# Sample attention of a four-layer encoder step: score products issued as one row, new keys as a 128-key block

## The chip, the core and the metric

The program runs on one core of a Trainium2 chip. The core has a matrix engine (TensorE: PE in the profile, with its weight loads as PEld), three engines for elementwise work (VectorE: DVE, ScalarE: ACT, GpSimd: POOL) and a queue that issues the DMA transfers (SyncE: SP). Each engine works through its own instructions in the order in which the program lists them and waits on semaphores. The metric is the device time of one execution in microseconds; lower is better.

## What is computed

One inference step of four transformer layers of width 2048, for 256 prompt tokens and for 8 batch elements with 16 new tokens each ("sample"). Layer i mixes by kind i mod 3: band attention with sinks (A, layers 0 and 3), latent attention (B, layer 1), chunk-band attention (C, layer 2). Beside the mixer, every layer has a 4-head cross-attention into 256 memory tokens. The sample half attends to cached keys and to the 16 new keys of its own batch element:

```python
def attend(q, k, v, bias, valid, sink):
    s = jnp.einsum("bqhgd,bkhd->bhgqk", qg, k) * (d ** -0.5)
    if bias is not None:
        s = s + bias
    ...
    p = jax.nn.softmax(s, axis=-1)      # kind A adds the sink to the denominator
    return jnp.einsum("bhgqk,bkhd->bqhgd", p, v)

# kinds A and C, sample: cached keys first, then the new ones
out = attend(q, concat([past_k, k], axis=1), concat([past_v, v], axis=1), bias_fn(rel), None, sink)
y = x + (concat([out, cross]) * silu(gate)) @ w_out
```

The numbers of cached keys are 128 (A), 512 (B and C) and 256 (cross).

## The kernel before

All large products (`proj_nat`, `proj_tr`) split both operands into two parts and run three products of 128 contraction rows by 128 columns of weights each. Their weights come by DMA (`raw_*`), are split by ACT (`whi_*`, L149) and DVE (`wlo_*`, L150), two buffers of each, and go to PE. The program is written as a data flow with tiles and pools; a planner decides, before the kernel is built, in which order each engine gets its instructions, so that attention work and large products alternate on PE. Pools bound how far things run ahead: `kcT` (transposed keys) has four buffers, `prs` (scores and probabilities, one row per query and head) two, `cch` (cached keys and values) five, the PSUM bank `s` one.

TensorE can be addressed in parts. A product with 32 queries as weights (`128*32` in the profile: 128 contraction rows, 32 columns) takes a quarter of the array's columns; which quarter follows from where the result starts in PSUM (`s[32 * h:32 * h + 32]`). With 32 contraction rows (`32*32`, `32*64`, `32*128`) it also takes a quarter of the rows. A product of two fp32 operands shows as two MATMUL instructions.

The sample attention, for each kind:

- **C** (`layer_c`, L695 to L740): three groups of four heads, eight batch elements, 24 blocks in all. Per block: for each head four transposes of cached keys (L707) into `ktp`, a copy to `kcT` (DVE for even heads, ACT for odd ones) and directly behind it that head's score product (L714); then softmax; four transposes of the probabilities `pt`; the new keys' probabilities; 16 products with the cached values (L734) and four with the new ones (L737); one transpose of the result. Where the next group's projections or the gate products are ready, the planner puts them between.
- **A** (`sample_a`, two layers, two pairs of key heads, four pairs of batch elements: 16 blocks). Eight score products with 64 columns of queries (`128*64`), half with 128 cached keys and half with 16 new ones; two transposes of probabilities; products with values for each of two batch elements and two key heads: cached (L597), then new (L598).
- **B** (`sample_b`, eight batch elements, two halves of the heads): 96 rows of queries and heads, 512 cached latents, and the new ones at L1059 and L1067.
- **Cross** (`cross`, L440 to L472): 16 blocks of two batch elements, per element four score products of 256 keys (L451).

The new keys of batch elements 2n and 2n+1 share 32 partitions (16 each) of the tiles that hold all eight elements' new values (`vn[:, 2]`, `c_s`). `new_block` (L387) lays a block of 32 probabilities next to the cached ones, the 16 of the own element and 16 zeros for the neighbour (POOL memset, L392). Those 32 columns are turned into rows by a product with the identity (`mm(o[vr, P:256], blk, ident)`, L587, L727, L1059), which writes the 32 partitions `vr` where the new values lie, and the product with the new values has 32 contraction rows (`ptn[vr]` by `vn[vr]`, L598, L737, L1067).

Of the kernel before, what the change touches and what calls it, by code (L numbers as in the profile page):

```python
# [10 lines left out]
F32 = mybir.dt.float32  # L11
# [48 lines left out]
def encoder_step(ctx: ExitStack, tc: tile.TileContext, ins: dict, outs: list, layers=(0, 1, 2, 3)):  # L60
# [73 lines left out]
    # ---------------------------------------------------------------- products  # L134
# [65 lines left out]
    # ---------------------------------------------------------------- residual stream  # L200
# [28 lines left out]
    # column k of the residual stream, transposed, and its squares  # L229
# [27 lines left out]
    # ---------------------------------------------------------------- memory keys and values  # L257
# [50 lines left out]
    # ---------------------------------------------------------------- attention, prompt  # L308
# [19 lines left out]
    def attn_band(nm, qk, v0, v1, bm, sink, dst, mul=False):  # L328
# [6 lines left out]
        pr = sm.tile([P, 544], F32, tag="prs", name=f"pr_{nm}")  # L335
# [21 lines left out]
    def attn_full(nm, q, k, v0, v1, dst, mul):  # L357
        s = atb(f"s_{nm}", "o")
        for t in range(2):
            mm(s[:, t * 256:(t + 1) * 256], q[:, t * P:(t + 1) * P], k)  # L360
        nmx = tiny.tile([P, 4], F32, tag="nm", name=f"nm_{nm}")
        nc.vector.tensor_reduce(nmx[:, :2], s.rearrange("p (t k) -> p t k", t=2), AX.X, ALU.max, negate=True)
        pr = sm.tile([P, 544], F32, tag="prs", name=f"pr_{nm}")
# [52 lines left out]
    def cross(l, xqT, oT, mul=False):  # L416
# [23 lines left out]
        for b2 in range(NB // 2):  # L440
# [13 lines left out]
            pr = sm.tile([P, 544], F32, tag="prs", name=f"pr_{nm}")  # L454
# [19 lines left out]
    # ---------------------------------------------------------------- gate and output projection  # L474
# [8 lines left out]
    # silu(2u) = u (1 + tanh u), rbc holds half the scale  # L483
# [62 lines left out]
    # ---------------------------------------------------------------- layers  # L546
    def sample_a(l, j, p2, qs, kT, vn, sink_r, oT):
# [7 lines left out]
        for b2 in range(4):  # L555
            nm = f"as{l}{p2}{b2}"
            vr = slice(32 * b2, 32 * b2 + 32)
# [6 lines left out]
            pr = sm.tile([P, 544], F32, tag="prs", name=f"pr_{nm}")  # L564
            bl = []
            for i in range(2):
                b = 2 * b2 + i
                bl.append(new_block(pr[:, i * 160:(i + 1) * 160], P, b))
                po, no = (0, P) if i == 0 else (DS, 0)
                for jj in range(2):  # L570
# [3 lines left out]
                    mm(s[rows, i * 144 + po:i * 144 + po + P], q, kcT[:, (2 * i + jj) * P:(2 * i + jj + 1) * P])  # L574
                    mm(s[rows, i * 144 + no:i * 144 + no + DS], q, kT[:, kv, SP0 + DS * b:SP0 + DS * (b + 1)])
            nmx = tiny.tile([P, 4], F32, tag="nm", name=f"nm_{nm}")
            for i in range(2):
                bo = DS if i == 0 else 0
                nc.vector.tensor_tensor_reduce(out=bl[i][3], in0=s[:, i * 144:(i + 1) * 144], in1=bm_a[:, p2, bo:bo + 144],
                                               scale=-1.0, scalar=sink_r[:, 2 + p2:3 + p2], op0=ALU.add, op1=ALU.min,  # L580
                                               accum_out=nmx[:, i:i + 1])
# [7 lines left out]
            nc.scalar.copy(pts[:, 0:256], pt[:, 0:256])  # L589
            nc.vector.tensor_copy(pts[vr, 256:512], pt[vr, 256:512])  # L590
            o = atb(f"o_{nm}", "o")
            for i in range(2):
                for jj in range(2):
                    kv = 2 * p2 + jj
                    c0 = i * P + 64 * jj
                    oo = o[64 * jj:64 * jj + 64, i * P:(i + 1) * P]
                    mm(oo, pts[:, c0:c0 + 64], vcs[b2 // 2][:, 2 * (b2 % 2) + i, jj * P:(jj + 1) * P], True, False)  # L597
                    mm(oo, pts[vr, 256 + c0:256 + c0 + 64], vn[vr, 2, kv * P:(kv + 1) * P], False, True)  # L598
# [59 lines left out]
    def layer_c(l, xt, rx, xres, last):  # L658
# [3 lines left out]
        for g in range(3):  # L662
# [32 lines left out]
            for b in range(NB):  # L695
# [6 lines left out]
                vr = slice(32 * (b // 2), 32 * (b // 2) + 32)  # L702
                s = atb(f"s_{nm}", "s")
                for h in range(4):
# [9 lines left out]
                    mm(s[32 * h:32 * h + 32, :], q, kcT)  # L714
                pr = sm.tile([P, 544], F32, tag="prs", name=f"pr_{nm}")
                past, new, blk, span = new_block(pr, 512, b)
# [13 lines left out]
                ptn = sm.tile([P, P], F32, tag="ptn", name=f"ptn_{nm}", bufs=1)  # L730
                nc.vector.tensor_copy(ptn[vr], o[vr, P:256])
                for kt in range(4):
                    for h in range(4):
                        mm(o[32 * h:32 * h + 32, 0:P], pts[:, kt * P + 32 * h:kt * P + 32 * h + 32],  # L734
                           vc[kt // 2][:, kt % 2, h * P:(h + 1) * P], kt == 0, False)
                for h in range(4):
                    mm(o[32 * h:32 * h + 32, 0:P], ptn[vr, 32 * h:32 * h + 32], vn[vr, 2, h * P:(h + 1) * P], False, True)  # L737
# [5 lines left out]
    # ---------------------------------------------------------------- latent attention  # L743
# [12 lines left out]
    def layer_b(l, xt, rx, xres, last):  # L756
# [7 lines left out]
        # new latents and rotary keys  # L764
# [30 lines left out]
        # query latents, memory queries, gates  # L795
# [27 lines left out]
        # [latent half][head half]: batch, head, position  # L823
# [6 lines left out]
        def two_heads(qc):  # L830
# [21 lines left out]
            # absorbed sample queries  # L852
# [29 lines left out]
            # keys and values of two heads  # L882
# [62 lines left out]
        # key products, only for the norms of the cached keys  # L945
# [13 lines left out]
        # one row per head to one row per head and query  # L959
# [52 lines left out]
        def sample_b(b, rk, ch, cl, raw, krT):  # L1012
            nm = f"bs{b}"
            vr = slice(32 * (b // 2), 32 * (b // 2) + 32)
# [18 lines left out]
            ptn = qkp.tile([P, 1552], F32, tag="kT", name=f"ptn{nm}")[vr, 0:192]  # L1033
            for hf in range(2):
# [12 lines left out]
                pr = sm.tile([P, 544], F32, tag="prs", name=f"pr_{nm}{hf}")  # L1047
                past, new, blk, span = new_block(pr[:96], 512, b)
# [11 lines left out]
                mm(pt[vr, 384:480], blk, ident[:96, :96])  # L1060
                nc.scalar.copy(ptb[:, :, hf * 96:(hf + 1) * 96], pt[:, 0:384].rearrange("p (t r) -> p t r", t=4))
                nc.vector.tensor_copy(ptn[:, hf * 96:(hf + 1) * 96], pt[vr, 384:480])
# [11 lines left out]
        # scores of the new latents: 32 keys of two batch elements at a time, of which the own ones are kept  # L1074
# [48 lines left out]
    # ---------------------------------------------------------------- gains and biases  # L1123
# [6 lines left out]
    def setup():  # L1130
# [13 lines left out]
        # relative-position biases: one row per head over rel in descending order  # L1144
# [16 lines left out]
        # every head's row once per query, so that a row pitch of one less shifts it by one per query  # L1161
# [10 lines left out]
        bm_a = cst.tile([P, 2, 160], F32, name="bm_a")  # L1172
        nc.gpsimd.memset(bm_a, 0.0)
        for p2 in range(2):
            for j in range(2):
                r, h0 = slice(j * 64, j * 64 + 48), 6 * p2 + 3 * j
                nc.sync.dma_start(out=bm_a[r, p2, DS:160], in_=toeplitz(sh_a, h0, 127, [[LA * 64, 3], [LA - 1, DS], [1, 144]]))
                nc.sync.dma_start(out=bm_a[r, p2, 0:DS], in_=toeplitz(sh_a, h0, 255, [[LA * 64, 3], [LA - 1, DS], [1, DS]]))
# [19 lines left out]
    # ---------------------------------------------------------------- run  # L1198
# [63 lines left out]
```

## Time and profile before

| | |
|---|---|
| median of 3 runs | 2983.43 us (2979.32 to 2983.58) |
| profiled execution, first to last instruction | 2979.2 us |
| PE busy | 2945.2 us, 99% of the span |
| DVE, ACT, POOL busy | 1351.6, 1315.1, 422.8 us |
| DMA engines busy, mean | 46.4% |
| granted TensorE clock, mean | 0.996 of full speed |

In the rows of the timeline below, a line is one instruction or several equal ones in a row (xN): its start, the time until the last of them ends, engine, line, operation, tile written<-tiles read, and the form rows*columns of the array with the size of the moving operand. Ends of matmuls are modelled and overlap with what follows, so what one line costs PE is read from its start to the start of the next line.

### The profile page before, as it was taken

To read this page: it belongs to the slowest core of one execution; us is meant where nothing else is said; L and a number is where in the kernel's file an instruction comes from. 1 tells how busy PE (TensorE), PEld (TensorE's weight loads), DVE (VectorE), ACT (ScalarE), POOL (GpSimd) and SP (SyncE) were. 2 spreads that over 40 slices of the span, in tenths; PEclk is the share of its full clock that TensorE was granted. 3 is DMA by queue.
4 is the path that set the end of the run, shared out by engine and by line. 5 is a ranking of instruction groups with operands and counts; after the bars stand their busy time and mean duration, and the time that the engine had idled before them with its cause. 6 is when DMAs were issued, how large, how long until landed. Compare 5 with 4: busy or idle time off the path is not lost.

```text
span 2979.2 us, 44016 instructions
## 1 busy us (share of the span) xinstructions
PE 2945.2 (99%) x17178; PEld 2499.4 (84%) x17178; DVE 1351.6 (45%) x2521; ACT 1315.1 (44%) x2819; POOL 422.8 (14%) x437
## 2 busy tenths in 40 slices
PE   8989999999999999999999999999999999999999
PEld 6867888899989987888898877777889987888987
DVE  5544445453434455555443443343445344345433
ACT  6555355333444365444334453434334344553332
POOL 1100111011100063333011110010101111010100
PEclk9999999999999999999999999999999999999999
DMA  7785553354444622001444546655566444532343
GB/s 256 240 271 184 169 163 100 113 184 149 147 131 121 186 78 61 16 23 56 162 149 131 163 158 215 203 175 197 175 198 223 149 138 128 189 108 89 111 163 130
DMA packets 314830, 446.82 MB, mean 150 GB/s; under 512 B 20833, under 2 KB 183666, under 8 KB 314622
## 3 DMA queue, kind: packets, MB, share of 16 engines
q1 hardware_dynamic: 314622, 444.01, 46.4%
q8 instruction: 135, 2.21, 0.3%
q14 instruction: 73, 0.60, 0.1%
HBM read 412.48 MB, written 34.69 MB: 150 GB/s over the span
## 4 chain that ended last, share of the span: by engine, by line
PE 96%; DMA 2%; DVE 1%; ACT 1%; SPq 0%; issue 0%; DVEq 0%; ACTq 0%
PE pt_g L90 18%; PE pt_o L90 13%; PE pn_aq L90 7%; PE kpkn L90 5%; PE pn_o L90 4%; PE pn_m L90 4%; PE pn_xq L90 4%; PE pn_cq L90 3%; PE pn_ck L90 3%; PE pn_cv L90 3%; PE pn_ak L90 2%; PE pn_av L90 2%; PE s_cs L90 2%; PE ktpcs L103 2%; PE o_as L90 2%; PE o_cs L90 1%
## 5 line engine op out<-in xcount | busy, mean ns | idle before, releaser
L90 PE MATMUL pt_g<-xt_x,whi_g 128*128 128x384 f32 x2048 | 534.4, 341 | 0.0
L90 PE MATMUL pt_o<-og,whi_o 128*128 128x384 f32 x1536 | 379.2, 334 | 0.0
L90 PEld LDWEIGHTS pt_g<-xt_x,whi_g 128*128 128x128 f32 x2048 | 367.8, 188 | 13.2 <-issue 11.6
L90 PE MATMUL pt_g<-xt_x,wlo_g 128*128 128x384 f32 x1024 | 343.4, 343 | 0.0
L150 DVE TENSOR_TENSOR wlo_o<-raw_o,whi_o 128x1024 fp32r<-128x1024 f32 x128 | 157.7, 1232 | 262.9 <-ACT whi_o L149 259.4
L90 PEld LDWEIGHTS pt_o<-og,whi_o 128*128 128x128 f32 x1536 | 276.3, 188 | 0.2 <-issue 0.2
L149 ACT CAST whi_o<-raw_o 128x1024 fp32r<-128x1024 f32 x128 | 134.6, 1052 | 278.9 <-PE pt_o L90 148.6
L90 PE MATMUL pt_o<-og,wlo_o 128*128 128x384 f32 x768 | 245.6, 335 | 0.0
L150 DVE TENSOR_TENSOR wlo_g<-raw_g,whi_g 128x1024 fp32r<-128x1024 f32 x128 | 160.4, 1253 | 176.7 <-ACT whi_g L149 171.3
L149 ACT CAST whi_g<-raw_g 128x1024 fp32r<-128x1024 f32 x128 | 134.3, 1049 | 183.8 <-PE pt_g L90 154.6
L90 PEld LDWEIGHTS pt_g<-xt_x,wlo_g 128*128 128x128 f32 x1024 | 191.9, 188 | 7.7 <-issue 6.8
L90 PE MATMUL pn_aq<-whi_aq,xt_x 128*128 128x512 f32 x576 | 186.2, 399 | 0.0
L90 PE MATMUL pn_m<-whi_m,xt_m 128*128 128x512 f32 x512 | 161.6, 395 | 0.4 <-ACT whi_m L154 0.4
L90 PEld LDWEIGHTS pt_o<-og,wlo_o 128*128 128x128 f32 x768 | 143.2, 188 | 0.0
L90 PE MATMUL kpkn<-wk,chkn 128*128 128x384 f32 x512 | 133.5, 343 | 0.0
L155 DVE SCALAR_TENSOR_TENSOR wlo_m<-raw_m,gc_mem,whi_m 128x512 fp32r<-128x512 f32 x128 | 97.6, 803 | 76.0 <-ACT whi_m L154 76.0
L90 PEld LDWEIGHTS pn_aq<-whi_aq,xt_x 128*128 128x128 f32 x576 | 107.0, 188 | 22.5 <-issue 0.8
L90 PE MATMUL pn_xq<-whi_xq,xt_x 128*128 128x512 f32 x384 | 122.0, 395 | 0.5 <-ACT xt_x L214 0.5
L90 PE MATMUL pn_o<-whi_o,og 128*128 128x512 f32 x384 | 119.6, 391 | 0.0
L90 PE MATMUL pn_aq<-wlo_aq,xt_x 128*128 128x512 f32 x288 | 115.2, 401 | 0.0
L90 PEld LDWEIGHTS pn_m<-whi_m,xt_m 128*128 128x128 f32 x512 | 95.8, 189 | 21.1 <-ACT whi_m L154 1.1
L154 ACT ACTIVATE whi_m<-raw_m,gc_mem 128x512 fp32r<-128x512 f32 x128 | 85.8, 716 | 58.6 <-PE pn_m L90 58.2
(502 smaller groups left out, 5974.9 us busy)
## 6 DMA issues: line engine op xcount, KB each, us to landing
raw_o<-in_w_out_dram SPq DMA_DIRECT2D x128, 512.0 KB
raw_m<-in_w_mem_kv_dram SPq DMA_DIRECT2D x64, 512.0 KB
raw_g<-in_a_w_in_dram SPq DMA_DIRECT2D x64, 512.0 KB
raw_aq<-in_a_w_in_dram SPq DMA_DIRECT2D x48, 512.0 KB
kccs<-in_cache_c_k_dram SPq DMA_DIRECT2D x48, 512.0 KB
vccs<-in_cache_c_v_dram SPq DMA_DIRECT2D x48, 512.0 KB
kxs<-in_cache_mem_k_dram SPq DMA_DIRECT2D x32, 512.0 KB
vxs<-in_cache_mem_v_dram SPq DMA_DIRECT2D x32, 512.0 KB
```

The costliest lines, as they stand in the source:

```text
L90: nc.tensor.matmul(out, lhsT=lhsT, rhs=rhs, start=start, stop=stop)
L103: nc.tensor.transpose(out, in_, ident[:k, :k])
L149: nc.scalar.copy(hi[:, :, :ncols], r)
L150: nc.vector.tensor_tensor(lo[:, :, :ncols], r, hi[:, :, :ncols].bitcast(F32), ALU.subtract)
L154: nc.scalar.activation(hi[:, i, :ncols], r[:, i, :], AF.Copy, scale=g)
L155: nc.vector.scalar_tensor_tensor(lo[:, i, :ncols], r[:, i, :], g, hi[:, i, :ncols].bitcast(F32), ALU.mult, ALU.subtract)
```

## The change

- A helper `mm_row` issues a list of products so that all of them come behind the first on PE. The cross-attention and kind C put the last head first (its keys are transposed last); in C, the four score products of a block are now issued after all four transposes and copies. The products with the values and A's scores go through it as well.
- `new_block` now makes a block of 128 columns behind the cached keys: all of it is filled (POOL memset of 128 columns in place of 16) with a value whose exponential is zero, and the element's own 16 scores are written over it by the DVE. The softmax runs over the whole of it (640 columns in place of 528 in B and C, 256 in place of 144 in A).
- The block is transposed like the cached keys' probabilities (128 by 128), and its product with the new values has 128 contraction rows, all eight elements' new keys, of which seven have probability zero.
- In A the score and bias step becomes two DVE instructions per batch element (16 new and 128 cached columns) in place of one; the copy of transposed probabilities becomes one ACT copy of 512 columns in place of an ACT copy of 256 and a DVE copy of 256; `bm_a` loses its second copy of 16 columns and four small loads.
- `ptn` in C moves from a buffer of its own to the pool's `osb` buffers (two); `prs` grows from 544 to 640 columns.

```diff
     def mm(out, lhsT, rhs, start=True, stop=True):
-        nc.tensor.matmul(out, lhsT=lhsT, rhs=rhs, start=start, stop=stop)
+        return nc.tensor.matmul(out, lhsT=lhsT, rhs=rhs, start=start, stop=stop)
...
-    def new_block(pr, n, b):
-        if b % 2 == 0:
-            past, new, blk, zero, span = 0, n, n, n + DS, 0
-        else:
-            past, new, blk, zero, span = 2 * DS, DS, 0, 0, DS
-        nc.gpsimd.memset(pr[:, zero:zero + DS], 0.0)
-        return pr[:, past:past + n], pr[:, new:new + DS], pr[:, blk:blk + 2 * DS], pr[:, span:span + n + DS]
+    def new_block(pr, n, b, fill):
+        blk = pr[:, n:n + P]
+        nc.gpsimd.memset(blk, fill)
+        return pr[:, 0:n], pr[:, n + DS * b:n + DS * (b + 1)], blk, pr[:, 0:n + P]
+
+    def mm_row(calls):
+        first = mm(*calls[0])
+        with tc.issue_after(first.ins):
+            for c in calls[1:]:
+                mm(*c)
...
# cross
-                for h in range(4):
-                    mm(s[32 * h:32 * h + 32, i * 256:(i + 1) * 256], xqT[:, h, c0:c0 + 32], mkT[h])
+                mm_row([(s[32 * h:32 * h + 32, i * 256:(i + 1) * 256], xqT[:, h, c0:c0 + 32], mkT[h]) for h in (3, 2, 1, 0)])
...
# sample_a: eight score products in one mm_row; softmax over pr[:, 0:256] and pr[:, 256:512]
             for i in range(2):
-                tr(pt[:, i * P:(i + 1) * P], bl[i][0])
-                mm(pt[vr, 256 + i * P:256 + (i + 1) * P], bl[i][2], ident)
+                for c in range(2):
+                    tr(pt[:, (2 * i + c) * P:(2 * i + c + 1) * P], pr[:, (2 * i + c) * P:(2 * i + c + 1) * P])
...
-                for jj in range(2):
-                    ...
-                    mm(oo, pts[:, c0:c0 + 64], vcs[b2 // 2][:, 2 * (b2 % 2) + i, jj * P:(jj + 1) * P], True, False)
-                    mm(oo, pts[vr, 256 + c0:256 + c0 + 64], vn[vr, 2, kv * P:(kv + 1) * P], False, True)
+                for c in range(2):
+                    for jj in range(2):
+                        kv = 2 * p2 + jj
+                        c0 = (2 * i + c) * P + 64 * jj
+                        v = vn[:, 2, kv * P:(kv + 1) * P] if c else vcs[b2 // 2][:, 2 * (b2 % 2) + i, jj * P:(jj + 1) * P]
+                        row.append((o[64 * jj:64 * jj + 64, i * P:(i + 1) * P], pts[:, c0:c0 + 64], v, c == 0, c == 1))
+            mm_row(row)
...
# layer_c
-                    mm(s[32 * h:32 * h + 32, :], q, kcT)
+                    row.insert(0, (s[32 * h:32 * h + 32, :], q, kcT))
+                mm_row(row)
...
-                mm(o[vr, P:256], blk, ident)
+                tr(o[:, P:256], blk)
...
-                for h in range(4):
-                    mm(o[32 * h:32 * h + 32, 0:P], ptn[vr, 32 * h:32 * h + 32], vn[vr, 2, h * P:(h + 1) * P], False, True)
+                for h in range(4):
+                    row.append((o[32 * h:32 * h + 32, 0:P], ptn[:, 32 * h:32 * h + 32], vn[:, 2, h * P:(h + 1) * P], False, True))
+                mm_row(row)
...
# sample_b
-                mm(pt[vr, 384:480], blk, ident[:96, :96])
+                tr(pt[:, 384:480], blk)
...
-                mm(o[:, a * 192:(a + 1) * 192], c_s[vr, a * P:(a + 1) * P], ptn, False, True)
+                mm(o[:, a * 192:(a + 1) * 192], c_s[:, a * P:(a + 1) * P], ptn, False, True)
```

## Rows read from the trace of the kernel before

**Rows 1.** The page: busy time of the engines, and the chain that ended last.

```profile
PE 2945.2 (99%) x17178; PEld 2499.4 (84%) x17178; DVE 1351.6 (45%) x2521; ACT 1315.1 (44%) x2819; POOL 422.8 (14%) x437
PE 96%; DMA 2%; DVE 1%; ACT 1%; SPq 0%; issue 0%; DVEq 0%; ACTq 0%
```

**Rows 2.** Windows, C: stretch, length, PE PEld DVE ACT POOL busy, clock, DMA share, GB/s.

```profile
1774.00:2262.00 488.00, 488.00 (x3510) 371.31 (x3509) 204.80 (x408) 193.65 (x395) 46.50 (x57) 1.00 0.59 192
```

**Rows 3.** Timeline of PE: C, one head's score product by itself.

```profile
2053.36 0.33 PE L90 MATMUL pt_g<-xt_x,wlo_g 128*128 128x384 f32 x1
2053.62 1.05 PE L90 MATMUL s_cs<-kcTcs,qTc 128*32 128x512 f32 x2
2054.60 0.62 PE L90 MATMUL pt_g<-xt_x,whi_g 128*128 128x384 f32 x2
2055.06 0.35 PE L90 MATMUL pt_g<-xt_x,wlo_g 128*128 128x384 f32 x1
2055.24 0.52 PE L90 MATMUL pt_g<-xt_x,whi_g 128*128 128x384 f32 x2
```

**Rows 4.** Timeline of PE: C, value products, then four heads' scores.

```profile
2082.18 1.08 PE L90 MATMUL o_cs<-vccs,pts_cs 128*32 128x128 f32 x32
2083.19 0.42 PE L90 MATMUL o_cs<-nat_cv,ptn_cs 32*32 32x128 f32 x8
2083.54 1.06 PE L90 MATMUL s_cs<-kcTcs,qTc 128*32 128x512 f32 x8
2084.54 0.44 PE L90 MATMUL pt_g<-xt_x,wlo_g 128*128 128x384 f32 x1
```

**Rows 5.** Timeline of PE: first and last of C's 55 stretches of scores.

```profile
1778.96 1.05 PE L90 MATMUL s_cs<-kcTcs,qTc 128*32 128x512 f32 x2
...
2243.78 1.04 PE L90 MATMUL s_cs<-kcTcs,qTc 128*32 128x512 f32 x2
```

**Rows 6.** Timeline of PE: C, probabilities of the new keys by an identity product.

```profile
2059.32 0.60 PE L103 MATMUL pt_cs<-identr,pr_cs 128*128 128x128 f32 x4
2059.85 0.41 PE L90 MATMUL o_cs<-identr,pr_cs 128*32 128x128 f32 x2
2060.19 0.33 PE L103 MATMUL ktpcs<-identr,kccs 128*128 128x128 f32 x1
```

**Rows 7.** Timeline of PE: A, eight value products, then another block's transposes.

```profile
494.31 0.43 PE L90 MATMUL o_as<-av,pts_as 128*64 128x128 f32 x2
494.67 0.43 PE L90 MATMUL o_as<-nat_av,pts_as 32*64 32x128 f32 x2
...
497.19 0.33 PE L103 MATMUL pt_as<-identr,pr_as 128*128 128x128 f32 x1
497.45 0.41 PE L90 MATMUL pt_as<-identr,pr_as 128*32 128x128 f32 x2
```

**Rows 8.** Timeline of PE: A, score products.

```profile
466.65 0.45 PE L90 MATMUL s_as<-kcTas,qs 128*64 128x128 f32 x4
466.92 0.25 PE L90 MATMUL s_as<-kT,qs 128*64 128x16 f32 x4
```

**Rows 9.** Timeline of PE: cross, one head's scores, and four heads'.

```profile
276.72 0.62 PE L90 MATMUL s_xs<-mkTxs,xqT 128*32 128x256 f32 x2
...
360.79 0.64 PE L90 MATMUL s_xs<-mkTxs,xqT 128*32 128x256 f32 x8
```

**Rows 10.** Timeline of PE: B, value product of the new keys, and the cached ones.

```profile
1232.01 0.59 PE L90 MATMUL o_bs<-ptnbs,keep 32*128 32x192 f32 x2
1232.52 1.57 PE L90 MATMUL o_bs<-ptbbs,ckvkn 128*128 128x192 f32 x8
```

**Rows 11.** Timeline of ACT and of DVE in C; by line: POOL's memsets of `pr`.

```profile
2078.63 0.59 ACT L729 COPY pts_cs<-pt_cs 128x512 f32<-128x512 f32 x1 [0.20 <-PE pt_cs L103]
...
2060.62 0.17 DVE L718 CUSTOM_DVE_ANT_0 pr_cs<-sn,bmcs 128x16 f32<-128x16 f32 x1
...
L392 POOL MEMSET pr_cs<- 128x16 f32 x24 | 2.7, 112 | 226.8 <-PE o_cs L90 201.9 <-ACT pts_cs L729 13.5 <-PE pt_c L103 8.2
```

More of the change, by code (lines that the diff above doesn't have):

```diff
@@ L563, in sample_a @@
             s = atb(f"s_{nm}")
-            pr = sm.tile([P, 544], F32, tag="prs", name=f"pr_{nm}")
-            bl = []
+            row = []
             for i in range(2):
                 b = 2 * b2 + i
-                bl.append(new_block(pr[:, i * 160:(i + 1) * 160], P, b))
-                po, no = (0, P) if i == 0 else (DS, 0)
                 for jj in range(2):
@@ L573, in sample_a @@
                     q = qs[:, b * 192 + kv * 48:b * 192 + kv * 48 + 64]
-                    mm(s[rows, i * 144 + po:i * 144 + po + P], q, kcT[:, (2 * i + jj) * P:(2 * i + jj + 1) * P])
-                    mm(s[rows, i * 144 + no:i * 144 + no + DS], q, kT[:, kv, SP0 + DS * b:SP0 + DS * (b + 1)])
+                    row.append((s[rows, i * 144:i * 144 + P], q, kcT[:, (2 * i + jj) * P:(2 * i + jj + 1) * P]))
+                for jj in range(2):
+                    kv = 2 * p2 + jj
+                    rows = slice(64 * jj, 64 * jj + 64)
+                    q = qs[:, b * 192 + kv * 48:b * 192 + kv * 48 + 64]
+                    row.append((s[rows, i * 144 + P:(i + 1) * 144], q, kT[:, kv, SP0 + DS * b:SP0 + DS * (b + 1)]))
+            mm_row(row)
+            pr = sm.tile([P, 640], F32, tag="prs", name=f"pr_{nm}")
+            bl = [new_block(pr[:, i * 256:(i + 1) * 256], P, 2 * b2 + i, -LOW) for i in range(2)]
             nmx = tiny.tile([P, 4], F32, tag="nm", name=f"nm_{nm}")
             for i in range(2):
-                bo = DS if i == 0 else 0
-                nc.vector.tensor_tensor_reduce(out=bl[i][3], in0=s[:, i * 144:(i + 1) * 144], in1=bm_a[:, p2, bo:bo + 144],
+                nc.vector.tensor_tensor_reduce(out=bl[i][1], in0=s[:, i * 144 + P:(i + 1) * 144], in1=bm_a[:, p2, P:144],
                                                scale=-1.0, scalar=sink_r[:, 2 + p2:3 + p2], op0=ALU.add, op1=ALU.min,
+                                               accum_out=nmx[:, 2 + i:3 + i])
+                nc.vector.tensor_tensor_reduce(out=bl[i][0], in0=s[:, i * 144:i * 144 + P], in1=bm_a[:, p2, 0:P],
+                                               scale=-1.0, scalar=nmx[:, 2 + i:3 + i], op0=ALU.add, op1=ALU.min,
                                                accum_out=nmx[:, i:i + 1])
@@ L585, in sample_a @@
             for i in range(2):
-                tr(pt[:, i * P:(i + 1) * P], bl[i][0])
-                mm(pt[vr, 256 + i * P:256 + (i + 1) * P], bl[i][2], ident)
+                for c in range(2):
+                    tr(pt[:, (2 * i + c) * P:(2 * i + c + 1) * P], pr[:, (2 * i + c) * P:(2 * i + c + 1) * P])
             pts = sm.tile([P, 512], F32, tag="pts", name=f"pts_{nm}")
-            nc.scalar.copy(pts[:, 0:256], pt[:, 0:256])
-            nc.vector.tensor_copy(pts[vr, 256:512], pt[vr, 256:512])
+            nc.scalar.copy(pts, pt)
             o = atb(f"o_{nm}", "o")
+            row = []
             for i in range(2):
-                for jj in range(2):
-                    kv = 2 * p2 + jj
-                    c0 = i * P + 64 * jj
-                    oo = o[64 * jj:64 * jj + 64, i * P:(i + 1) * P]
-                    mm(oo, pts[:, c0:c0 + 64], vcs[b2 // 2][:, 2 * (b2 % 2) + i, jj * P:(jj + 1) * P], True, False)
-                    mm(oo, pts[vr, 256 + c0:256 + c0 + 64], vn[vr, 2, kv * P:(kv + 1) * P], False, True)
+                for c in range(2):
+                    for jj in range(2):
+                        kv = 2 * p2 + jj
+                        c0 = (2 * i + c) * P + 64 * jj
+                        v = vn[:, 2, kv * P:(kv + 1) * P] if c else vcs[b2 // 2][:, 2 * (b2 % 2) + i, jj * P:(jj + 1) * P]
+                        row.append((o[64 * jj:64 * jj + 64, i * P:(i + 1) * P], pts[:, c0:c0 + 64], v, c == 0, c == 1))
+            mm_row(row)
             for i in range(2):
@@ L701, in layer_c @@
                         nc.sync.dma_start(out=ts[i], in_=I[src][0, b, 256 * i:256 * i + 256, hs, :].rearrange("(t p) h d -> p t (h d)", p=P))
-                vr = slice(32 * (b // 2), 32 * (b // 2) + 32)
                 s = atb(f"s_{nm}", "s")
+                row = []
                 for h in range(4):
@@ L713, in layer_c @@
                     q = qT[:, h, SP0 + DS * b:SP0 + DS * b + 32]
-                    mm(s[32 * h:32 * h + 32, :], q, kcT)
-                pr = sm.tile([P, 544], F32, tag="prs", name=f"pr_{nm}")
-                past, new, blk, span = new_block(pr, 512, b)
+                    row.insert(0, (s[32 * h:32 * h + 32, :], q, kcT))
+                mm_row(row)
+                pr = sm.tile([P, 640], F32, tag="prs", name=f"pr_{nm}")
+                past, new, blk, span = new_block(pr, 512, b, -LOW)
                 nmx = tiny.tile([P, 4], F32, tag="nm", name=f"nm_{nm}")
@@ L1032, in sample_b @@
             ptb = slot(f"ptb{nm}").rearrange("p (t r) -> p t r", t=4)
-            ptn = qkp.tile([P, 1552], F32, tag="kT", name=f"ptn{nm}")[vr, 0:192]
+            ptn = qkp.tile([P, 1552], F32, tag="kT", name=f"ptn{nm}")[:, 0:192]
             for hf in range(2):
@@ L1046, in sample_b @@
                 nc.scalar.copy(rs[:96, 0:512], r[:96])
-                pr = sm.tile([P, 544], F32, tag="prs", name=f"pr_{nm}{hf}")
-                past, new, blk, span = new_block(pr[:96], 512, b)
+                pr = sm.tile([P, 640], F32, tag="prs", name=f"pr_{nm}{hf}")
+                past, new, blk, span = new_block(pr[:96], 512, b, LOW)
                 mx = tiny.tile([P, 4], F32, tag="mx", name=f"mx_{nm}{hf}")
@@ L1176, in setup @@
                 r, h0 = slice(j * 64, j * 64 + 48), 6 * p2 + 3 * j
[L1177 to L1178 removed]
+                nc.sync.dma_start(out=bm_a[r, p2], in_=toeplitz(sh_a, h0, 127, [[LA * 64, 3], [LA - 1, DS], [1, 144]]))
         yield
```

22 lines of the change are left out of this document (11 added, 11 removed).

## Prediction, made before the changed kernel ran

> **What bounds the kernel now.** I read three views. First the busy times and the chain that ended last [rows 1]: PE is busy 99% of the span and makes up 96% of the chain, while DVE and ACT are near 45%. Next the windows of the stretch where most of the changed work lies, layer C's sample attention [rows 2]: PE 488 of 488 us, DVE 205, ACT 194, the DMA engines 0.59 busy, clock 1.00. So nothing but PE's own work sets the time there; what it no longer does is gained, as long as the others keep pace. "Busy" says little about what an instruction costs, since matmuls overlap, so the third view is the timeline of PE, read from the start of one line to the start of the next.
>
> There, three things are to be seen. (1) Going to another form of the array costs time on both sides. In a run of `pt_g`, one product takes 0.18 us (2055.06 to 2055.24); the one ahead of a 128\*32 product takes 0.26 (2053.36 to 2053.62), and the first two behind it 0.46 in place of 0.36 [rows 3]. So an excursion into another form costs about 0.09 to go and 0.05 to 0.10 to return, beside its work. (2) A score product of one head takes 0.98 us [rows 3], and those of four heads in a row 1.00 us (2083.54 to 2084.54) [rows 4]: four quarters of the array work at once. (3) Each hop between 128 and 32 contraction rows costs as well: A's eight value products, alternating between the two forms, take 2.88 us (494.31 to 497.19), 0.36 each [rows 7]; four A score products in one form and on two halves of the array, the same work in two products, take 0.27 us (466.65 to 466.92) [rows 8].
>
> **The change part by part.** All savings are of PE, against the profiled execution of 2979.2 us.
>
> *C, scores in a row.* The timeline has 55 stretches of these products [rows 5]: 28 of one head by itself, 4 of two heads, 20 right behind a block's value products (of these, 8 with all four heads), 3 among the new keys' score products. In a row, 24 remain, most of them behind value products, since both wait for the same thing: the copy out of the one bank `s`. 31 stretches go, each 0.98 + 0.09 + 0.10 = 1.17 us: **36 us**.
>
> *C, block of new keys.* The identity product takes 0.34 us, and the four transposes ahead of it 0.53 in place of 0.44 [rows 6]; with the return it is near 0.50. In its place comes a fifth transpose in the same form, a quarter of that 0.44, 0.11: 24 times 0.39, **9 us**. The four value products take 0.35 us, and the sixteen ahead 1.01, of which 0.09 is the hop [rows 4]. In one form each group of four instructions adds 1.01 - 0.09 over eight groups, some 0.11, so the ten groups take near 1.14 in place of 1.36: 24 times 0.22, **5 us**.
>
> *A.* Four pairs of value products in a row cost 4 times 0.22, plus the entry and the return, near 1.0 us in place of 2.88 [rows 7, 8]: 16 times 1.88, **30 us**. A transpose and its identity product take 0.26 + 0.34 us [rows 6, 7], two such per block, 1.2; four transposes take 0.44: 16 times 0.76, **12 us**. The scores are in longer stretches, but four of each eight have only 16 columns; some of their 16 blocks are broken up now, for 0 to 5 us; I take **2**.
>
> *Cross.* One head's scores last as long as those of four (0.62 and 0.64 us) [rows 9]. For the first two batch elements of each layer there are five stretches instead of two; three go, each 0.55 us plus 0.2 for the excursion, in four layers: **9 us**. The other elements' heads stand in a row already.
>
> *B.* The new keys' value product takes 0.51 us (1232.01 to 1232.52) plus 0.19 of hops; as two instructions in the form of the cached ones (eight took 1.5 us, less 0.19 for the hops: 0.16 each) 0.33 [rows 10]: 16 times 0.37, 6 us. Its identity product has 96 columns, and costs at most what C's does (0.50) and at least the hops (0.15); against a transpose of 0.08 this is 1 to 7 us, and I take 6, being nearer to C's. Together **12 us**.
>
> Sum: 36 + 9 + 5 + 30 + 12 + 2 + 9 + 12 = **115 us**.
>
> *What is added elsewhere.* Exponentials run over 112 more columns, 72 times: 0.1 us each on ACT by C's 0.7 us for 528. A's second score step is 32 small DVE instructions of 0.17 to 0.3 us, against 16 DVE copies that go; its ACT copy is 0.2 us longer. POOL fills 128 columns in place of 16 (0.112 us [rows 11]; at most three times that). Four small loads go. These engines are idle half of the time in that stretch [rows 2], and the PE order leaves room: `pts_cs` ended at 2079.22 and PE took it up at 2082.18 [rows 4, 11]. I cost them at nothing; without that cover, 0.3 us in each of 56 blocks would be 17 us.
>
> *The added waits.* (a) The first product of a row needs the last head's copy, so all of the PE queue behind it waits if that copy is late. (b) The DVE instruction that writes the new scores (L718 in C) now waits for POOL's memset of the same columns; behind it on DVE queue the `wlo` splits that PE needs. Neither can gain, since both only add a condition; what they may cost is in the rivals. (c) `ptn` waits for an `osb` buffer, whose last reader is the value products or the closing transpose of the block before, both ahead in PE's order.
>
> A rule of the Trainium skill speaks against the row of heads. The trace shows four heads, eight instructions of full height, taking 1.00 us together [rows 4]. "TensorE: Matmul & The Clock Gate", section "The mechanism", holds that weight loads overlap running matmuls only where the row group differs; all heads of such a row have the same four row groups. By that rule the loads would stand between the products, and a row would gain little. The row of four that is already in this trace decides against it.
>
> **The rivals.**
> 1. *The rows come apart.* The edit only says that three products come behind the first; the planner may put `pt_g` between. Then the C scores and cross gain nothing: 115 - 45 = 70 us, **2913**. Against it: their operands are ready together, and 8 of the 20 stretches behind value products already hold four heads.
> 2. *A chain becomes late.* With PE faster, waits for copies, exponentials and splits come to light, about 1 us in each of 56 blocks (the room was 3 us in the block that I read): near **2920**. For it: DVE and ACT work the same in less time. Against: when PE frees buffers sooner, their work starts sooner too.
> 3. *Slower: DVE stands behind POOL.* In C, POOL sat idle 227 us before its 24 memsets, 202 of them for a `pr` buffer that PE had yet to give back [rows 11]. If such a memset is queued behind other POOL waits when DVE already wants the columns, DVE stops, the two `wlo` buffers run out, and PE stops. It decides from 115 / 24 = 4.8 us of PE wait in each C block; at 9.5 us, the mean of those POOL waits, it would be 24 x 4.7 = 113 us above the present, **3096**. Against: DVE's L718 shows no wait of its own in the row read, and the planner orders it and the memset alike.
> 4. *More than that.* The planner uses the shorter chains to close the last gaps, and value products and scores share more excursions: near **2850**.
>
> **How the numbers follow.** 2979.2 - 115 = 2864. The median run lies 4 us above the profiled execution: 2868; the terms' roundings and the A scores allow 2 more of gain: **2866**. Chances: forecast (2855 to 2885) 0.68, rival 1 0.07, rival 2 0.14, rival 3 0.03, rival 4 0.06, gains lost altogether 0.02. Leaving out both ends, the range is **2846 to 2908**. A measurement of this kernel tells about 0.2% from no change. Faster by more than that 0.95, within it 0.02, slower 0.03.
>
> **What would show it.** In the profile after: `s_cs` in 24 stretches of eight instructions, about 1.0 us each; no 32-row forms in `o_as`, `o_cs`, `o_bs`; `o_as` near 1.0 us per block; five `pt`-like transposes per C block at 0.11; PE still 99% busy and C's stretch some 50 us shorter. Wrong would be: PE idle time ahead of `s_cs` or `pt_g` named for DVE or POOL (rivals 2, 3), stretches of two or four instructions left (rival 1), or a row of four heads longer than 1.0 us.

## The result, and the profile after

The changed kernel takes **2871.3 us** (median of 4 runs, 2867.0 to 2873.3) against 2983.4 us before: a ratio of 0.9627, 95% interval 0.9613 to 0.9642. A second set of runs gave 2872.2 us and the same ratio. The prediction was 2866 (2846 to 2908), so it held; 5 us of the 117 promised did not come, and most of what follows is about those and about whether the rest came for the reasons given.

The page after, in the lines that answer to [rows 1]: busy time of the engines, and shares of the chain that ended last.

```profile
PE 2837.7 (99%) x17106; PEld 2484.1 (87%) x17106; DVE 1345.5 (47%) x2569; ACT 1322.9 (46%) x2819; POOL 425.7 (15%) x437
PE 96%; DMA 2%; DVE 1%; ACT 1%; SPq 0%; issue 0%; DVEq 0%; ACTq 0%
```

The span is 2870.2 us, 109.0 less. PE's busy time fell by 107.5 us although only 72 of its 17178 instructions went: what went is time between starts, not work. PE is idle 32.5 us (34.0 before), so nothing new came to light behind it. The window of the whole of layer C up to its output projection (columns as in [rows 2]) says the same of the stretch with the largest gain; it took 697.5 us before.

```profile
1535.50:2180.20 644.70, 643.48 (x4626) 537.70 (x4624) 284.38 (x536) 292.38 (x617) 72.19 (x75) 1.00 0.60 198
```

PE 643.5 of 644.7 us, DVE and ACT below half: still PE alone.

**By layer.** The table takes, from the timeline of PE, the time from the first product of `pn_xq` of a layer to the first one of its output projection (`pt_o`, `pn_o` in the last), in the profiled execution of each kernel. What lies between (memory keys, output projections) differs by 4 us at most in any of them. The experiments are described below.

| us | layer 0 (A) | layer 1 (B) | layer 2 (C) | layer 3 (A) |
|---|---|---|---|---|
| before | 455.7 | 560.6 | 697.3 | 436.1 |
| only C's rows | 456.0 | 560.9 | 664.9 | 436.1 |
| only cross rows | 451.1 | 559.6 | 694.4 | 433.7 |
| only the block of new keys | 435.7 | 550.9 | 680.5 | 417.0 |
| after | 433.3 | 550.0 | 644.7 | 414.6 |
| after, profiled again | 432.2 | 546.9 | 644.0 | 414.6 |

The two rows of the changed kernel show how far one execution differs from another: 1 us in layers 0 and 2, 3 us in layer 1. Where a finer reading is needed below, it is taken *by tile*: every PE instruction is charged with the time from its start to the start of the next one, waits of more than 0.15 us are left out, and the charges are added up over a layer by the tile written. In the two executions of the changed kernel the sums named below agree to 0.2 us.

**What each edit looks like now.** The timeline of PE, columns as in the rows of before. First C, from three places: a row of scores by itself; value products and a row behind them; the transposes of the probabilities, the fifth (`o_cs<-identr,pr_cs`) behind the four.

```profile
1777.28 1.07 PE L90 MATMUL s_cs<-kcTcs,qTc 128*32 128x512 f32 x8
1778.28 0.74 PE L90 MATMUL pn_cv<-whi_cv,xt_x 128*128 128x512 f32 x2
...
1855.13 1.08 PE L90 MATMUL o_cs<-vccs,pts_cs 128*32 128x128 f32 x32
1856.03 0.40 PE L90 MATMUL o_cs<-nat_cv,ptn_cs 128*32 128x128 f32 x8
1856.24 1.04 PE L90 MATMUL s_cs<-kcTcs,qTc 128*32 128x512 f32 x8
...
1862.64 0.60 PE L103 MATMUL pt_cs<-identr,pr_cs 128*128 128x128 f32 x4
1863.07 0.27 PE L103 MATMUL o_cs<-identr,pr_cs 128*128 128x128 f32 x1
1863.10 0.94 PE L90 MATMUL pn_ck<-whi_ck,xt_x 128*128 128x512 f32 x3
```

Eight instructions of a score row take 1.00 us (1777.28 to 1778.28), close to the 0.98 that two took in [rows 3]. The twenty value products take 1.11 us (1855.13 to 1856.24) in place of the 1.36 of [rows 4]: the 32-row form and its hop are gone. The fifth transpose starts 0.43 us behind the first of the four, as the next product did in [rows 6] less a hop, and nothing changes form behind it.

A, a block's value products; then cross, one row of scores; then B, the new values and what follows.

```profile
474.10 0.44 PE L90 MATMUL o_as<-av,pts_as 128*64 128x128 f32 x4
474.37 0.39 PE L90 MATMUL o_as<-nat_av,pts_as 128*64 128x128 f32 x4
474.59 0.39 PE L90 MATMUL o_as<-av,pts_as 128*64 128x128 f32 x4
474.81 0.39 PE L90 MATMUL o_as<-nat_av,pts_as 128*64 128x128 f32 x4
475.12 0.44 PE L103 MATMUL pt_as<-identr,pr_as 128*128 128x128 f32 x2
...
288.80 0.64 PE L90 MATMUL s_xs<-mkTxs,xqT 128*32 128x256 f32 x8
289.37 0.50 PE L90 MATMUL pn_av<-whi_av,xt_x 128*128 128x512 f32 x1
...
1234.94 0.49 PE L90 MATMUL o_bs<-ptnbs,keep 128*128 128x192 f32 x2
1235.27 0.98 PE L90 MATMUL o_bs<-ptbbs,ckvkn 128*128 128x192 f32 x5
```

A's eight value products take 1.02 us (474.10 to 475.12) in place of 2.88 [rows 7], and nearly the same in all 16 blocks; B's new keys 0.33 in place of 0.51 and two hops [rows 10]; four heads of the cross scores last 0.64 us, where one head lasted 0.62 [rows 9].

Not all went well. A's scores, at two places of the same pair of key heads:

```profile
462.49 0.44 PE L90 MATMUL s_as<-kcTas,qs 128*64 128x128 f32 x4
462.76 0.24 PE L90 MATMUL s_as<-kT,qs 128*64 128x16 f32 x4
462.85 0.42 PE L90 MATMUL s_as<-kcTas,qs 128*64 128x128 f32 x4
463.10 0.24 PE L90 MATMUL s_as<-kT,qs 128*64 128x16 f32 x4
...
469.04 0.38 PE L103 MATMUL pt_as<-identr,pr_as 128*128 128x128 f32 x2
469.35 0.43 PE L90 MATMUL s_as<-kcTas,qs 128*64 128x128 f32 x2
469.72 0.44 PE L103 MATMUL pt_as<-identr,pr_as 128*128 128x128 f32 x2
470.08 0.32 PE L90 MATMUL s_as<-kcTas,qs 128*64 128x128 f32 x1
...
470.86 0.44 PE L90 MATMUL pt_g<-xt_x,whi_g 128*128 128x384 f32 x1
```

The first block's row is whole. In the second, the planner issued the first product (469.35) and then put two transposes of an older block between it and the other seven: two excursions in place of one. This happens in 10 of the 16 blocks and makes 28 stretches of A's scores, where there were 24 before and 16 are possible.

### The profile page after: what moved, and what is told of

Same layout as the page of the kernel before. It is cut to its first block, busy times and chain, and to the rows that moved or that the text cites. A ratio compares the mean times of both kernels' runs of the same rounds, so it can differ in the third digit from the quotient of the medians.

```text
span 2870.2 us, 43881 instructions
## 1 busy us (share of the span) xinstructions
PE 2837.7 (99%) x17106; PEld 2484.1 (87%) x17106; DVE 1345.5 (47%) x2569; ACT 1322.9 (46%) x2819; POOL 425.7 (15%) x437
## 4 chain that ended last, share of the span: by engine, by line
PE 96%; DMA 2%; DVE 1%; ACT 1%; SPq 0%; issue 0%; DVEq 0%; ACTq 0%
PE pt_g L90 19%; PE pt_o L90 14%; PE pn_aq L90 7%; PE kpkn L90 5%; PE pn_o L90 5%; PE pn_m L90 4%; PE pn_xq L90 4%; PE pn_cv L90 3%; PE pn_ck L90 3%; PE pn_cq L90 3%; PE pn_av L90 2%; PE pn_ak L90 2%; PE ktpcs L103 2%; PE s_bs L90 1%; PE pn_bqb L90 1%; PE pn_bq L90 1%
```

## The experiments

Theory: time is the sum of PE's starts. An excursion from the array's full form (a stretch of products in a smaller form) costs near 0.19 us beside its work, quarters or halves of the array work side by side only while the form stays, and what the change adds on DVE, ACT and POOL is hidden. The first three kernels split the change in parts, the others test single reasons.

**C's rows alone**, from the kernel before (with the helper `mm_row`):

```diff
-                    mm(s[32 * h:32 * h + 32, :], q, kcT)
+                    row.insert(0, (s[32 * h:32 * h + 32, :], q, kcT))
+                mm_row(row)
```

> The kernel before with one edit: layer C's four score products stand in a row behind the last head's copy; the new keys keep their block of 32 rows. My theory (each stretch of score products costs TensorE near 1.17 us however many heads stand in it, so 31 stretches fewer are 36 us): 2983 - 36 = 2947 us (2942 to 2954), s_cs in some 24 to 26 stretches of eight instructions at 1.0 us. Rival (the row makes the softmax of each block start later, and TensorE waits): 2960 to 2983, with idle time of PE ahead of pt_cs or o_cs. Rival (the rows come apart without the rest of the change): s_cs in about 50 stretches and 2983.

2951.3 us, ratio 0.9898 (0.9883 to 0.9913): 32 us gained, 26 to 35 by the interval. The scores stand in 26 stretches, nearly all of eight instructions; 29 fewer at 1.17 us would be 34, and layer 2 is 32.4 us shorter. No wait took the place: both rivals fall for C.

**Cross rows alone**, from the kernel before (with the helper `mm_row`):

```diff
-                for h in range(4):
-                    mm(s[32 * h:32 * h + 32, i * 256:(i + 1) * 256], xqT[:, h, c0:c0 + 32], mkT[h])
+                mm_row([(s[32 * h:32 * h + 32, i * 256:(i + 1) * 256], xqT[:, h, c0:c0 + 32], mkT[h]) for h in (3, 2, 1, 0)])
```

> The kernel before with one edit: the cross attention's four score products stand in a row. My theory (three excursions of one head fewer in each of four layers, 0.75 us each): 2983 - 9 = 2974 us (2971 to 2978), s_xs in some 26 stretches in place of 44. Rival (they were in time that nothing else used): 2983.

2974.3 us, ratio 0.9973 (0.9964 to 0.9982): 9 us, as expected. Excursions with `s_xs` go from 36 (not 44, as I had counted) to 25, and layers 0, 2 and 3 are each 2 to 5 us shorter.

**The block of new keys alone**: the changed kernel with these two rows taken back (the two diffs above, reversed).

> The changed kernel without the rows of score products in C and in the cross attention; what stays is the 128-key block of new keys in A, B and C with its value products in one form. My theory (the savings add up: 115 less 36 less 9): 2983 - 70 = 2913 us, and 2913 to 2920 as A's score rows come apart in the trace after. Rival (the two parts need each other, since only a block in one form lets a row of scores stand right behind the value products): 2930 or more, and then the first two runs give less than 36 and 9 as well.

2912.6 us, ratio 0.9768 (0.9755 to 0.9781): 71 us. The three parts add to 32 + 9 + 71 = 112 us, the whole gave 112: within the intervals, of up to 5 us either way, no part needs another.

**Which head is first**, from the changed kernel:

```diff
-... for h in (3, 2, 1, 0)])
+... for h in range(4)])
...
-                    row.insert(0, (s[32 * h:32 * h + 32, :], q, kcT))
+                    row.append((s[32 * h:32 * h + 32, :], q, kcT))
```

> The changed kernel with the heads of each row in C and in the cross attention in the order 0, 1, 2, 3 in place of 3, 2, 1, 0: the row's first product is now the one whose operands are ready first. My theory (being named together does nothing, the gain comes from the first product being the one that is ready last, so that the others have nothing to wait for): the rows come apart, s_cs in some 52 stretches and s_xs in 44, and 36 + 9 us less the few kept are lost: 2900 to 2920 us. Rival (it is enough that three products stand behind the first): 2871, with 24 stretches.

2910.3 us, ratio 0.9755 (0.9742 to 0.9769), the time of the kernel without these rows (2912.6). Timeline of PE in C:

```profile
1778.96 1.05 PE L90 MATMUL s_cs<-kcTcs,qTc 128*32 128x512 f32 x2
1779.94 0.66 PE L103 MATMUL ktpcs<-identr,kccs 128*128 128x128 f32 x4
1780.52 1.04 PE L90 MATMUL s_cs<-kcTcs,qTc 128*32 128x512 f32 x2
```

One head's score, the next head's transposes, the next score: as before. Over the whole kernel `s_cs` stands in 51 stretches and `s_xs` in 36; without these rows it was 56 and 36. `mm_row` only sets an order behind the first product. What makes a row is that the first one named is the one whose operands are ready last. This is the rival "rows come apart" of the prediction, made to happen: it costs 39 us, against 45 in the prediction.

**32 rows again**, from the changed kernel: the new keys' value products read only the 32 partitions of the own pair; order and number of all products stay.

```diff
+                        vr = slice(32 * b2, 32 * b2 + 32) if c else slice(0, P)
-                        ... vn[:, 2, kv * P:(kv + 1) * P] if c ... pts[:, c0:c0 + 64]
+                        ... vn[vr, 2, kv * P:(kv + 1) * P] if c ... pts[vr, c0:c0 + 64]
```

(C: `ptn[vr]` by `vn[vr]`; B: `c_s[vr]` by `ptn[vr]`.)

> The changed kernel with one thing undone: the value products of the new keys read 32 rows again in A, B and C (the block's other rows are zero); order and number of all products stay. My theory (each change between 128 and 32 contraction rows costs about 0.1 us and keeps products of the two forms from overlapping): C one change per block, 0.2 us, 24 times, 5 us; A three changes inside each row of eight products and a longer way back, 0.3 to 0.6 us, 16 times, 5 to 10 us; B 0.37 us, 16 times, 6 us: 2871 + 16 to 21 = 2887 to 2892 us. Rival (the hops are free, and all of the value products' gain came from putting the two halves of the array side by side): 2871. Rival (the hops were all of A's 30 us): 2871 + 5 + 30 + 6 = 2912.

2890.5 us, ratio 0.9691 (0.9675 to 0.9707), 18 us above the changed kernel on the same chip (2872.2): inside the theory's 16 to 21. One block of A in this kernel:

```profile
548.05 0.44 PE L90 MATMUL o_as<-av,pts_as 128*64 128x128 f32 x4
548.42 0.43 PE L90 MATMUL o_as<-nat_av,pts_as 32*64 32x128 f32 x4
548.78 0.44 PE L90 MATMUL o_as<-av,pts_as 128*64 128x128 f32 x4
549.15 0.43 PE L90 MATMUL o_as<-nat_av,pts_as 32*64 32x128 f32 x4
549.52 0.55 PE L103 MATMUL pt_as<-identr,pr_as 128*128 128x128 f32 x3
```

1.47 us (548.05 to 549.52) against 1.02: three changes of form at 0.15 each. Over 16 blocks that is 7 us, which leaves 11 for C and B. By tile, `o_as` takes 7.1 us more than in the changed kernel, `o_cs` and `s_cs` 4.7, `o_bs` 4.9. Both rivals fall. In [rows 7] a change stood behind every product: the seven within a block are 1.05 us at that price, 17 us in 16 blocks. That leaves 0.8 us a block, 13 us in all, of the 30 gained: the two halves of the array, which work side by side here, did not do so there, since the form changed between any two products. (This split is worked out, not run by itself; the next experiment adds what it rests on.)

**Order of the halves**, from the changed kernel:

```diff
-                for c in range(2):
-                    for jj in range(2):
+                for jj in range(2):
+                    for c in range(2):
```

> The changed kernel with one order changed: in A's row of value products the cached and the new keys' product of one half of the array stand behind each other, where the changed kernel alternates between the two halves; form, number and rows stay. My theory (two products in a row overlap only if they use different halves): of eight products of 0.21 us each, six pairs no longer overlap fully, 0.5 to 0.8 us more in each of 16 blocks: 2871 + 8 to 13 = 2879 to 2884 us. Rival (without the hops the order does not matter): 2871.

2875.2 us, ratio 0.9642 (0.9625 to 0.9658), against 0.9627 (0.9613 to 0.9642): the intervals overlap, and 8 to 13 us are not there. My theory of this one fell. A block in its timeline:

```profile
545.93 0.45 PE L90 MATMUL o_as<-av,pts_as 128*64 128x128 f32 x4
546.20 0.40 PE L90 MATMUL o_as<-nat_av,pts_as 128*64 128x128 f32 x4
546.41 0.44 PE L90 MATMUL o_as<-av,pts_as 128*64 128x128 f32 x4
546.63 0.44 PE L90 MATMUL o_as<-nat_av,pts_as 128*64 128x128 f32 x4
547.00 0.66 PE L103 MATMUL pt_as<-identr,pr_as 128*128 128x128 f32 x4
```

1.07 us, 0.05 more than before the edit. With the kernel before and the one with 32 rows, all four combinations of form and order are now measured, per block: with changes of form 2.88 us in this order [rows 7] and 1.47 with the halves alternating, in one form 1.07 and 1.02. So the order matters only where the form changes.

In the order in which the built program lists PE's instructions, the cached and the new keys' product of one half stand together (`av`, `nat_av`, `av`, `nat_av`, two instructions each). By their starts on the chip all four `av` instructions run before any `nat_av`: the second half's first product starts 14 ns behind the first half's, ahead of the two `nat_av` instructions that stand before it. In one form, each half works through its own products and does not wait for the other's. (What was said ahead of the prediction, that an engine works in the order in which the program lists its instructions, holds for TensorE here only within one half.)

The Trainium skill, "TensorE: Matmul & The Clock Gate", section "The mechanism", has matmuls start and end strictly in program order; by that, the second half's first product could not start before both products of the first half. This trace differs in the starts (the ends are modelled), and the measurement decides. The Trainium skill, "TensorEngine Tiling (Array Packing)", section "Key Properties", says that different tiles can execute in parallel and that a change of the tiling mode drains the engine; this trace and the one with 32 rows are in line with it, with 0.05 us for the order and 0.15 us for each change.

**A's rows kept whole**, from the changed kernel:

```diff
-        with tc.issue_after(first.ins):
+        with tc.issue_after(first.ins), tc.high_priority():
```

> The changed kernel with the products of a row behind the first set ahead of everything else that is ready, so that A's score rows, of which 12 in 16 come apart in the trace after, stay whole. My theory (each split costs an excursion more, 0.5 us, 12 times): 2871 - 6 = 2865 us (2862 to 2868), s_as in 16 stretches in place of 28. Rival (the transposes that stood between only move, and the time is the same): 2871. Rival (the rows kept whole delay the older block's transposes and so its copy and value products): 2873 or more, with PE idle ahead of o_as.

(The 12 there are stretches above 16; they come from 10 blocks. The helper serves all rows, but only A's scores change their stretches.) 2868.5 us, ratio 0.9618 (0.9604 to 0.9632): 4 us less than the changed kernel beside it, which the intervals do not tell apart. The trace does:

```profile
471.19 0.38 PE L103 MATMUL pt_as<-identr,pr_as 128*128 128x128 f32 x2
471.50 0.44 PE L90 MATMUL s_as<-kcTas,qs 128*64 128x128 f32 x4
...
472.10 0.24 PE L90 MATMUL s_as<-kT,qs 128*64 128x16 f32 x4
472.27 0.44 PE L103 MATMUL pt_as<-identr,pr_as 128*128 128x128 f32 x2
472.47 0.42 PE L90 MATMUL pt_g<-xt_x,whi_g 128*128 128x384 f32 x1
```

The same two pairs of transposes and the row between them take 1.28 us (471.19 to 472.47); with the split it was 1.82 (469.04 to 470.86). 0.54 us for each of 12 splits would be 6.5 us; by tile, over all blocks, `s_as` takes 3.9 us less and `pt_as` 1.6, together 5.4. `s_as` stands in 16 stretches, and layer 3 is 2.9 us shorter (411.7), its half of that. Layer 0 (431.9) is only 1.4 us shorter: its `s_as` and `pt_as` fell by the same 2.7 us, but in this execution PE waited 8.3 us there for the load of `x_prompt`, against 6.3 in the changed kernel's. So in the time only a part is seen.

**B's other excursions**: the kernel above, and in B the cached keys' score products over 64 rotary rows use 128, the upper 64 zero.

```diff
+        for hf in range(2):
+            nc.gpsimd.memset(qrs[hf][64:P], 0.0)
...
-            kro = slot(f"kro{nm}")[:, 0:256].rearrange("p (t d) -> p t d", t=4)
+            kro = slot(f"kro{nm}")[:, 0:512].rearrange("p (t d) -> p t d", t=4)
+            nc.gpsimd.memset(kro[:, :, 64:P], 0.0)
...
-                mm(s[:96], qrs[hf][:64, b].rearrange("p h s -> p (h s)"), krT[:64], True, False)
+                mm(s[:96], qrs[hf][:, b].rearrange("p h s -> p (h s)"), krT, True, False)
...
-                mm(r[:96], spread[:, c], rT[:64])
+                mm(r[:96], spread[:, c], rT)
```

(The transposes that make `krT` and `rT` are 128 wide as well.)

> The kernel with A's rows kept whole, and one thing more: in B the score products over the 64 rotary rows (s_bs, r_bs) and the transposes that feed them use all 128 rows, the upper 64 filled with zeros, so that the cached keys' attention in B no longer leaves the form of its other products. My theory (a change of form costs near 0.19 us there and back, whatever its cause): the trace after has 26 such excursions of s_bs and r_bs, 26 times 0.19 is 5 us: 2868 - 5 = 2863 us (2860 to 2866). Rival (64 rows take less time than 128, or the fills and wider copies come late): 2868 or more.

**2858.3 us**, ratio 0.9587 (0.9573 to 0.9602), the fastest of all: by the ratios, since they ran on different chips, 9 us below the kernel it started from and 12 below the changed one; the intervals do not overlap, though the first pair's only just. The same place in the changed kernel, and then in this one:

```profile
1249.02 0.34 PE L90 MATMUL kpkn<-wk,clkn 128*128 128x384 f32 x1
1249.29 0.47 PE L90 MATMUL r_bs<-rTbs,spread 64*96 64x512 f32 x1
1249.59 1.02 PE L90 MATMUL s_bs<-krTkn,qrs 64*96 64x512 f32 x2
...
1252.02 0.51 PE L90 MATMUL kpkn<-wk,chkn 128*128 128x384 f32 x2
```

```profile
1243.25 0.34 PE L90 MATMUL kpkn<-wk,clkn 128*128 128x384 f32 x1
1243.42 0.39 PE L90 MATMUL r_bs<-rTbs,spread 128*96 128x512 f32 x1
1243.65 1.02 PE L90 MATMUL s_bs<-krTkn,qrs 128*96 128x512 f32 x2
...
1245.90 0.51 PE L90 MATMUL kpkn<-wk,chkn 128*128 128x384 f32 x2
```

From `kpkn` to `kpkn` 3.00 us before and 2.65 now: 0.35 for this half, in which the two products share one excursion; ten of the 16 halves have two, 26 excursions in all. Layer 1 is 8.1 us shorter than in the kernel it started from (550.5 to 542.4). Executions differ by 3 us there, but by tile `s_bs`, `r_bs` and the `kpkn` between them take 7.8 us less, 0.30 for each excursion: the gain is where it was expected, and the theory's 0.19 was too small for it.

**Eight fills**, from the changed kernel:

```diff
-        nc.gpsimd.memset(blk, fill)
+        for _ in range(8):
+            nc.gpsimd.memset(blk, fill)
```

> The changed kernel with POOL filling each block of new keys eight times in place of once, 7 x 0.2 us more ahead of the DVE step that writes the new scores. My theory (what is added on POOL, DVE and ACT lies beside TensorE's work): 2871 us (2867 to 2875). Rival (DVE stands behind POOL and TensorE behind both): 1.4 us in each of 24 C blocks and 16 of B's halves and 2.8 us in each of 16 A blocks is 101 us, 2972; if the order of the work leaves only half of it hidden, 2920.

2873.7 us, ratio 0.9640 (0.9624 to 0.9656): no difference that the intervals show, where 50 to 100 us would be seen. Groups by line: DVE's step that writes the new scores in the changed kernel, and then the same and POOL's fills with eight of them (the last numbers are idle time before the group and what ended it).

```profile
L729 DVE CUSTOM_DVE_ANT_0 pr_cs<-sn,bmcs 128x16 f32<-128x16 f32 x24 | 6.6, 283 | 0.6
```

```profile
L730 DVE CUSTOM_DVE_ANT_0 pr_cs<-sn,bmcs 128x16 f32<-128x16 f32 x24 | 6.6, 283 | 12.9 <-POOL pr_cs L391 12.5
L391 POOL MEMSET pr_cs<- 128x128 f32 x192 | 39.3, 205 | 195.9 <-PE o_cs L103 175.1 <-PE ktpcs L103 3.5 <-DVE wlo_cv L150 2.9
```

In the changed kernel DVE waits 0.6 us in all 24 blocks of C together, and no wait for POOL is named. With eight fills it does wait for POOL, 12.5 us, half a microsecond in each block, and PE does not notice. The new wait is there and has room.

**The changed kernel once more**, beside the kernels with 32 rows, with the other order and with A's rows kept whole:

> The changed kernel unaltered, beside the next three on the same chip: 2871 us (2867 to 2874) by its earlier runs.

2872.2 us, ratio 0.9627 (0.9613 to 0.9642).

## Why the prediction held, point by point

*PE alone sets the time.* Right: 99% busy before and after, 107.5 us of PE busy time gone for 109.0 us of span, and the rivals "a chain becomes late" and "DVE stands behind POOL" have no row for them. Costing the additions on DVE, ACT and POOL at nothing was right; the eight fills show that the cover is not thin for POOL and the DVE step behind it (ACT's longer exponentials were not varied by themselves).

*C's rows, 36 us.* 24 stretches of eight at 1.00 us, as said. By itself the edit gave 32 (26 to 35). One step was wrong: that most rows would stand behind value products. 11 of 24 do, where 20 of 55 stretches did, so 9 entries and returns near 0.2 us, some 2 us, came back.

*C's block, 9 + 5 us.* Layer 2 lost 16.8 us with the block alone, against 14 predicted; value products 1.11 us where 1.14 were predicted. Where the other 2 us come from was not taken apart.

*A, 30 + 12 + 2 us.* The value products are right to 1% (1.86 us saved in each of 16 blocks, 30 us). With the block alone the two A layers lost 20.0 and 19.1 us, 39 in place of 44. By tile, over both layers of the changed kernel, `o_as` takes 29.9 us less than before, `pt_as` 8.8 less in place of 12, and `s_as` 1.2 more in place of 2 less. So two terms are mis-sized by 3 us each, the transposes and the scores: I expected longer stretches of scores, and they were split further, 28 in place of 24. With the rows kept whole the three are 29.9, 10.4 and 2.7 us less, 43 of the 44; the splits cost the rest. This splitting is the prediction's first rival, which I had weighed for C and cross alone, at the one place where it happened. The argument against it, "their operands are ready together", holds in A too and was not enough: two transposes of an older block were issued ahead of the rest of the row. Set ahead of everything else, the rows stay whole. Why the planner does this in A and not in C was not tried.

*Why A's 30 us.* The prediction gave that each hop costs as well, 0.36 us for each product against four pairs at 0.22. The size was right, and the reason had two parts in one number: worked out from the 0.15 us for each change, 17 us are the changes themselves, 13 the two halves that could not work side by side.

*Cross, 9 us.* Measured 9.

*B, 12 us.* Layer 1 was 9.7 us shorter with the block alone, in a stage that differs by 3 between executions. By tile `o_bs` takes 4.9 us less, `pt_bs` 4.3 and `ctkn` behind it 0.7, where 6 and 6 were predicted. The value product is exact (0.33 us); what was sized too large is the hops around it, 0.30 us saved for each product in place of 0.37.

*The sum.* 115 predicted for the profiled execution, 109 measured there: A is 5 us short, C's rows 2 to 4, B 2, and C's block 3 over.

*The rule that spoke against it.* The row of four heads was weighed against the Trainium skill, "TensorE: Matmul & The Clock Gate", section "The mechanism", by which a row would gain little. With 24 such rows in C, 1.00 us in the one shown, the trace stands against that.

## What to carry to other kernels

Where the matrix engine is busy all the time, read its timeline from start to start and look for changes of the array's form: here an excursion cost 0.2 to 0.3 us there and back, a change inside a row 0.15 us, and more where it kept parts of the array from working side by side. Padding a small product with zeros to its neighbours' form was cheaper here than running it small, in each place where it was done. When products are to be issued in a row, put the one first whose operands are ready last, and look in the trace whether the rows are whole. Additions on other engines are free only as long as the matrix engine does not come to wait for them, so measure the cover once by making the addition several times larger.

## What was not expected of the hardware

- In one form of the array, the two halves do not hold each other to the program's order: a product of the second half started 14 ns behind the first half's, ahead of two instructions of the first half listed before it, and listing each half's products together cost only 0.05 us in a block of eight products.
- Zeros are cheaper than a change of form also where they fill half of the rows: B's scores over 64 rotary rows, from `kpkn` to `kpkn`, took 3.00 us, with 128 rows 2.65.
